# Retention's keys and values projected sooner; two gates and a query projected between the pairs of the lower half

## The chip, the core and the metric

The kernel runs on one core of a Trainium2 chip. The metric is the device time of one execution in microseconds (us), the median of several runs. The core has a matrix engine (TensorE, PE in the rows), three engines for element work (VectorE is DVE, ScalarE is ACT, GpSimd is POOL) and a queue from which most transfers are issued (SyncE, SP). Each engine works through its own instructions in the order in which they were built; an instruction that waits holds up all that stand behind it on that engine.

## The reference, cut to what matters

The input is x of 1024 rows by 1024 columns. It is normalised to u and multiplied with one wide weight matrix. The columns of the product are the inputs of three kinds of heads and of a gate:

```python
(dq, dk, dv, sq, ckv, iq, ik, iw, rq, rk, rv, gate) = jnp.split(proj, split_points, axis=-1)
o_a = diff_attention(dq, dk, dv, ...)        # 6 heads, difference of two softmaxes
o_b = dsa_attention(sq, rms_norm(ckv), iq, ik, iw, w_uk, w_uv, top_k)   # 6 heads, 256 best keys per query
o_c = retention(rotary(rq), rotary(rk), rv, ...)   # 4 heads, chunks of 128 rows with a running state
y = jax.nn.silu(gate) * concatenate([o_a, o_b, o_c])
h = h + y @ w_out;  return rms_norm(h, final_norm)
```

All is float32. The kernel multiplies in a reduced float format with both operands split into a high and a low part, so that each product takes three matmuls.

## The kernel before

**Projection units.** u lies in SBUF as `uh` and `ul` (high and low part, transposed). A unit projects a block of columns. It loads its weights from DRAM (tiles `wr`), GpSimd splits them into `wh` and `wl` (lines L119 and L123), and TensorE multiplies. The units of kind "b" (`g0` to `g7` for gates, `s0` to `s2` for the sparse queries, `q`, `k`, `ck`) have 48 matmuls of 512 columns (L130 to L132). The units `rq`, `rk`, `rv` of retention (kind "a") have 192 matmuls of 256 columns (L347 to L349). Results go back to DRAM: `gd` for gates, `qsq` for sparse queries, `rd` for retention; `rq` and `rk` are first rotated, two products on VectorE (L556, L557) and three on GpSimd (L559, L560, L563).

**Attention steps.** `attend` (L652) walks over 128-row blocks, one step each: scores on TensorE (L718 for differential attention, L787 and L788 for sparse), the row maximum on VectorE (L729, L795), the exponential on ScalarE, the division, transposes on TensorE (L678), their eviction on ScalarE (L113), and the product with the values on TensorE (L693). The steps are pipelined: scores of step t, transposes of step t-2. Differential attention has six sets of 8 steps (3 pairs of heads, 2 heads each). Sparse attention has, for each pair, 8 steps over the lower 512 rows (half 0) and 8 over the upper (half 1). `topk` and `ties` find the 256 best keys. One tie pass of a block is L490 to L495 on VectorE.

**Stages.** `run` (L898) makes four: the front; differential attention with `topk`, `ties` of blocks 3 and 2 and the units of `order` and `order2`; sparse attention over half 0 with the other ties, retention's blocks 0 to 3, the output weights and a first piece of the output projection; sparse attention over half 1 with retention's blocks 4 to 7 and two blocks of the output projection. The rest of the output projection ends the kernel.

**What sets the order.** `mix` (L46) interleaves streams by their costs and weights. What it makes is a priority: the tile scheduler then places each instruction by a simulated time line, so that matmuls of a unit and of the attention alternate finely. `order2` is a string of units; `M` stands for `up` and `ky` (values and keys of the sparse heads) mixed with the units of `mp`.

**Buffers that couple things.** The output weights `woh`, `wol` take the places of `uh`, `ul` (same tags, L964 and L965), so they can be written only when the last projection unit is through. Their 16 loads pass through two `wr` buffers, alternately split by ScalarE with VectorE and by GpSimd. The first projection piece (`project((7,), 0)`) needs `yr`, which SP loads too.

Of the kernel before, what the change touches and what calls it, by code (L numbers as in the profile page):

```python
# [28 lines left out]
    0, 384, 768, 1152, 1536, 1664, 2176, 2248, 2504, 2760, 3016)  # L29
WA = 384 + 72  # L30
C_R = (C_RQ, C_RK, C_RV)
K = {'mk': 'up ky', 'mp': 's2 g5 g4', 'rt': ('hl', 'pq'), 's0': ('gg', 'ag', 'gg', 'ag', 'gg', 'ag', 'gg', 'ag'), 'xp': 2, 'bufs': (8, 3, 3, 5, 3, 4, 1), 'pp': (7,), 'rot': 0, 'order': 'g0 g1 k1 q1 k2', 'order2': 'q2 g2 rq g6 s0 ck g7 s1 M g3 rv rk | ', 'wd': 36, 'wt': 13, 'wg': 119, 'gw': 56, 'rw': 26, 'rx': 132, 'pw': 40, 'ow': 84, 'nf': 2, 'ev': 200, 'late': 8, 'de': ('aa', 'aa', 'aa'), 'da': 'ax', 'gd': (7, 4, 2), 'hlp': 'sqkk', 'tkp': '', 'vt': 'v', 'rs': 'x', 'nv': 1, 'dn': 'v', 'ws': 'gg', 'oe': ('av', 'gg'), 'one': 0, 'idx': (42, 40), 'iqs': 'iq2 iq3 q0 k0'}
NST, NP, NPQ, NW, NHL, NHALF, NY = K["bufs"]


# [10 lines left out]
def mix(*streams):  # L46
    live = [[g, float(total), 0.0] for g, total in streams]
    while live:
        s = min(live, key=lambda v: v[2] / v[1])
        try:  # L50
            c = next(s[0])
            s[2] += c
            yield c
        except StopIteration:
            live.remove(s)


def interleave(*streams):
    for _ in mix(*streams):
        pass  # L60


def drain(*gens):
    for g in gens:
        for _ in g:
            pass


class Trunk:
# [260 lines left out]
    def evict(self, evac, *args):  # L330
        with self.tc.high_priority(offset=K["ev"]):
            evac(*args)
# [565 lines left out]
    def run(self):  # L898
# [24 lines left out]
        def seq(*gs):  # L923
            for g in gs:
                yield from g

        def units(s):
            return seq(*(unit(t) for t in s.split()))
# [4 lines left out]
        with self.tc.manual_schedule(engines={et.PE}):  # L933
# [6 lines left out]
                   (seq(self.topk(), self.ties((3, 2))), K["wt"]),  # L940
                   (units(K["order"] + " " + K["order2"].split("|")[0]), K["wg"]))
        self.v_load()
        interleave((seq(*(self.dsa(p, 0) for p in range(3))), 100), (self.ties((7, 6, 5, 4)), 110),
                   (seq(units(K["order2"].split("|")[1]), mix((self.retention(0), K["rw"]),
                                (seq(self.out_weights(), self.project(K["pp"], 0)), K["ow"]))), K["gw"]))
        interleave((seq(*(self.dsa(p, 1) for p in range(3))), 100),
                   (mix((self.retention(1), K["rx"]), (self.project(range(K["nf"])), 100)), K["pw"]))
        drain(self.project(range(K["nf"], 3)))
# [103 lines left out]
```

## Time and profile before

| | |
|---|---|
| median of 3 runs | 770.33 us (768.52 to 776.04) |
| profiled execution | 772.95 us, span 771.2 us, so 1.75 us lie outside the span |
| TensorE busy | 718.2 us (93%) |
| VectorE busy | 559.9 us (73%) |
| ScalarE busy | 458.6 us (59%) |
| GpSimd busy | 310.4 us (40%) |

A busy TensorE is not TensorE at its pace, since matmuls overlap in the records: one of 512 columns lasts 0.39 us there, while the next starts 0.23 us after it. What counts is how many starts a stretch has, and of what kind. The granted clock (1.00 is 2.4 GHz, and the lower level of 1.2 GHz pulls the mean down) stands beside each stretch.

### The profile page before, as it was taken

To read this page: it belongs to the slowest core of one execution; us is meant where nothing else is said; L and a number is where in the kernel's file an instruction comes from. 1 tells how busy PE (TensorE), PEld (TensorE's weight loads), DVE (VectorE), ACT (ScalarE), POOL (GpSimd) and SP (SyncE) were. 2 spreads that over 40 slices of the span, in tenths; PEclk is the share of its full clock that TensorE was granted. 3 is DMA by queue.
4 is the path that set the end of the run, shared out by engine and by line. 5 is a ranking of instruction groups with operands and counts; after the bars stand their busy time and mean duration, and the time that the engine had idled before them with its cause. 6 is when DMAs were issued, how large, how long until landed. Compare 5 with 4: busy or idle time off the path is not lost.

```text
span 771.2 us, 12824 instructions
## 1 busy us (share of the span) xinstructions
PE 718.2 (93%) x4266; PEld 591.1 (77%) x4266; DVE 559.9 (73%) x1315; ACT 458.6 (59%) x1002; POOL 310.4 (40%) x343
## 2 busy tenths in 40 slices
PE   6999999999989999978889889999978999999996
PEld 5986788887878988756767668989756887777884
DVE  3684577989999989999889986426657775654443
ACT  4762555489687877786845655533355665653332
POOL 6422122434424539447347787337633332120000
PEclk9999999999999999999899989999979999999998
DMA  9716455472484344451383685565579964413441
GB/s 337 255 28 178 137 159 142 111 191 79 118 202 109 99 132 113 114 144 31 91 239 108 172 229 167 145 203 165 177 212 272 251 203 113 132 34 106 137 166 55
DMA packets 93618, 116.73 MB, mean 151 GB/s; under 512 B 11120, under 2 KB 62704, under 8 KB 93424
## 3 DMA queue, kind: packets, MB, share of 16 engines
q1 hardware_dynamic: 91152, 111.94, 50.8%
q10 hardware_dynamic: 2400, 3.97, 1.4%
q8 instruction: 34, 0.56, 0.3%
q14 instruction: 32, 0.26, 0.1%
HBM read 79.17 MB, written 36.18 MB: 150 GB/s over the span
## 4 chain that ended last, share of the span: by engine, by line
PE 62%; DVE 13%; DMA 8%; issue 7%; ACT 4%; POOL 4%; SPq 2%; ACTq 0%; DVEq 0%; POOLq 0%
PE pG L130 6%; PE pG L131 6%; PE pG L132 6%; PE pB L693 5%; PE pB L678 4%; PE pG L1003 4%; PE pG L1004 4%; PE pG L1005 4%; PE pS L272 3%; PE pG L347 2%; DVE jv L443 2%; PE pG L349 2%; PE pG L348 2%; PE pS L409 2%; PE pS L408 2%
## 5 line engine op out<-in xcount | busy, mean ns | idle before, releaser
L130 PE MATMUL pG<-uh,wh 128*128 128x512 f32 x352 | 142.5, 405 | 4.5 <-DVE gt L894 2.1
L132 PE MATMUL pG<-uh,wl 128*128 128x512 f32 x352 | 141.2, 401 | 1.7 <-POOL wl L123 1.7
L131 PE MATMUL pG<-ul,wh 128*128 128x512 f32 x352 | 140.4, 399 | 1.3 <-DVE ul L255 1.3
L123 POOL TENSOR_TENSOR wl<-wr,wh 128x512 fp32r<-128x512 f32 x56 | 79.9, 1443 | 84.4 <-PE pG L131 73.8
L457 ACT ACTIVATE ja<-sc,tk_c 128x896 int8<-128x896 f32 (+2 forms) x93 | 83.3, 896 | 22.3 <-DVE tk_c L464 16.5
L113 ACT ACTIVATE pt<-pB 128x512 f32<-128x512 f32 (+2 forms) x120 | 58.9, 496 | 41.9 <-PE pB L678 41.7
L130 PEld LDWEIGHTS pG<-uh,wh 128*128 128x128 f32 x352 | 67.5, 192 | 19.3 <-DVE gt L894 2.4
L132 PEld LDWEIGHTS pG<-uh,wl 128*128 128x128 f32 x352 | 67.4, 192 | 16.7 <-POOL wl L123 2.5
L131 PEld LDWEIGHTS pG<-ul,wh 128*128 128x128 f32 x352 | 67.4, 191 | 15.5 <-DVE ul L255 3.3
L678 PE MATMUL pB<-ident,pp 128*128 128x128 f32 x432 | 73.4, 288 | 4.6 <-DVE gt L825 1.9
L693 PE MATMUL pB<-pt,v 128*64 128x128 f32 x864 | 68.0, 294 | 7.4 <-ACT pt L113 6.8
L693 PEld LDWEIGHTS pB<-pt,v 128*64 128x64 f32 x864 | 55.3, 143 | 18.9 <-ACT pt L113 9.5
L443 DVE TENSOR_SCALAR_CACHE_REDUCE jv<-sc,tk_c 128x640 bf16<-128x640 f32 (+4 forms) x81 | 69.1, 853 | 0.9
L119 POOL TENSOR_SCALAR wh<-wr 128x512 fp32r<-128x512 f32 x56 | 40.3, 723 | 69.9 <-DMA wr<-in_w_in_dram 50.8
L678 PEld LDWEIGHTS pB<-ident,pp 128*128 128x128 f32 x432 | 51.7, 145 | 20.4 <-issue 8.5
L744 POOL TENSOR_SCALAR pq<-pq,mx 128x896 f32<-128x896 f32 (+7 forms) x48 | 39.2, 816 | 58.5 <-DVE mx L743 46.1
L347 PE MATMUL pG<-wh,uh 128*128 128x256 f32 x192 | 55.4, 290 | 0.7 <-POOL wh L119 0.7
L411 ACT ACTIVATE pp<-pS 128x1024 f32<-128x1024 f32 (+5 forms) x48 | 36.5, 760 | 31.5 <-PE pS L409 31.5
L348 PE MATMUL pG<-wl,uh 128*128 128x256 f32 x192 | 55.0, 287 | 0.0
L349 PE MATMUL pG<-wh,ul 128*128 128x256 f32 x192 | 54.4, 284 | 0.0
L747 DVE SCALAR_TENSOR_TENSOR pp<-pp,mx,pq 128x896 f32<-128x896 f32 (+7 forms) x48 | 51.1, 1065 | 4.4 <-POOL pq L744 3.6
L416 DVE SCALAR_TENSOR_TENSOR sc<-pp,iw,sc 128x1024 f32<-128x1024 f32 (+5 forms) x42 | 43.5, 1048 | 14.6 <-ACT pp L411 14.2
(234 smaller groups left out, 1731.4 us busy)
## 6 DMA issues: line engine op xcount, KB each, us to landing
wr<-in_w_in_dram SPq DMA_DIRECT2D x56, 256.0 KB, 3.1
st<-qdq SPq DMA_DIRECT2D x24, 256.0 KB, 4.2
st<-qkk SPq DMA_DIRECT2D x18, 256.0 KB, 6.1
qiq<-hl SPq DMA_DIRECT2D x16, 256.0 KB, 3.5
st<-qiq SPq DMA_DIRECT2D x8, 512.0 KB, 3.4
wr<-in_w_out_dram SPq DMA_DIRECT2D x16, 256.0 KB, 3.3
xr<-in_x_dram SPq DMA_DIRECT2D x8, 512.0 KB, 3.6
yr<-yd SPq DMA_DIRECT2D x7, 512.0 KB, 4.1
```

The lines of the kernel that those rows point to most:

```text
L113: self.nc.scalar.activation(out, in_, AF.Copy)
L123: (self.nc.vector if e2 == "v" else self.nc.gpsimd).tensor_tensor(lo, src, hi.bitcast(F), OP.subtract)
L130: mm(ps, wh, xh, start=start, stop=False)
L131: mm(ps, wh, xl, start=False, stop=False)
L132: mm(ps, wl, xh, start=False, stop=stop)
L347: mm(ps, uh, hs[k], start=k == 0, stop=False)
L348: mm(ps, uh, ls[k], start=False, stop=False)
L349: mm(ps, ul, hs[k], start=False, stop=k == KC - 1)
L443: nc.vector.tensor_scalar(jv[:, :nv[b]], hb if b == 7 and bit >= 16 else sc[b], t, 0.0, op0=op, op1=OP.add, accum_out=cnt[:, j:j + 1])
L457: nc.scalar.activation(ja[:, :nv[b]], sc[b], AF.Sign, bias=cut(b), scale=-1.0, accum_out=cnt[:, cols[b]:cols[b] + 1])
L678: nc.tensor.transpose(p[:, k], pr[:, (k0 + k) * 128:(k0 + k + 1) * 128], self.ident)
L693: self.last = nc.tensor.matmul(o[u * 64:(u + 1) * 64], vals[k], pts[g, a][:, k, u * 128:(u + 1) * 128], start=k == (i if u else 0), stop=k ...
```

## The change

Three units leave the second stage and one table is written anew. In `order2` the second stage now has `q2 g2 rq s0 ck s1 M rk rv`, and `M` mixes `up ky` with `g3 g6 g7` (before: `s2 g5 g4`). The units `g4 s2` and `g5` now belong to the third stage. That stage, one call of `interleave` before, is now one call per pair of sparse heads: pair 0 with `g4 s2`, pair 1 with `g5`, pair 2 with nothing of the kind, each with a share of the ties and of retention's blocks; the output weights and the first piece of the projection come with pair 2. `rk` stands ahead of `rv` now.

```diff
-K = {..., 'mp': 's2 g5 g4', ..., 'order2': 'q2 g2 rq g6 s0 ck g7 s1 M g3 rv rk | ', ...}
+K = {..., 'mp': 'g3 g6 g7', ..., 'order2': 'q2 g2 rq s0 ck s1 M rk rv | g4 s2 | g5 | ', ...}
...
+def share(g, total):
+    while total > 0:
+        c = next(g, None)
+        if c is None:
+            return
+        total -= c
+        yield c
...
-        interleave((seq(*(self.dsa(p, 0) for p in range(3))), 100), (self.ties((7, 6, 5, 4)), 110),
-                   (seq(units(K["order2"].split("|")[1]), mix((self.retention(0), K["rw"]),
-                                (seq(self.out_weights(), self.project(K["pp"], 0)), K["ow"]))), K["gw"]))
+        ties, state = self.ties((7, 6, 5, 4)), self.retention(0)
+        side = K["order2"].split("|")[1:]
+        for p in range(3):
+            rest = mix((state, K["rw"]), (seq(self.out_weights(), self.project(K["pp"], 0)), K["ow"]))
+            interleave((self.dsa(p, 0), 33), (share(ties, 6), 30),
+                       (seq(units(side[p]), share(state, 4) if p < 2 else rest), 35))
+        drain(ties)
```

The built order shows what that makes. TensorE's instructions are the same as far as `rq`. Line numbers of the new kernel are 9 higher than before as far as `run` (13 higher in `project`). Before, TensorE went through the sparse steps of half 0 alone as soon as the last projection matmul (here at row 2252) was through; the scores are `pS`, the transposes take `ident`, the product with the values takes `pt` and `v`, and `rt` is retention's first block:

```order
2252 L349 MATMUL pG_5328<-wh_5085,ul 128x256
2253 L693 MATMUL pB_5796<-pt_5769,v_5586 64x128 x3
2254 L678 MATMUL pB_5820<-ident,pp_5778 128x128
2255 L787 MATMUL pS_5860<-st_5847,st_5848 128x512
2256 L788 MATMUL pS_5860<-st_5847,st_5848 128x512
2257 L787 MATMUL pS_5879<-st_5847,st_5848 128x128
2258 L788 MATMUL pS_5879<-st_5847,st_5848 128x128
2259 L678 MATMUL pB_5825<-ident,pp_5793 128x128 x2
2260 L693 MATMUL pB_5829<-pt_5819,v_5586 64x128 x3
2261 L678 MATMUL pB_5883<-ident,pp_5857 128x128 x3
2262 L787 MATMUL pS_5905<-st_5847,st_5848 128x256
2263 L788 MATMUL pS_5905<-st_5847,st_5848 128x256
```

Now the steps of pairs 0 and 1 have a unit between them; here it is the end of `g5`, with steps of pair 1:

```order
2268 L141 MATMUL pG_5957<-uh,wl_5796 128x512
2269 L139 MATMUL pG_5957<-uh,wh_5795 128x512
2270 L702 MATMUL pB_5854<-pt_5827,v_5367 64x128 x7
2271 L687 MATMUL pB_5885<-ident,pp_5836 128x128
2272 L796 MATMUL pS_5942<-st_5875,st_5876 128x128
2273 L797 MATMUL pS_5942<-st_5875,st_5876 128x128
2274 L140 MATMUL pG_5957<-ul,wh_5795 128x512
2275 L141 MATMUL pG_5957<-uh,wl_5796 128x512
2276 L139 MATMUL pG_5957<-uh,wh_5795 128x512
2277 L140 MATMUL pG_5957<-ul,wh_5795 128x512
```

After `g5`'s last matmul (row 2287) no unit is left, and TensorE has only the other steps and retention until the first matmul of the output projection (row 2413). In all, 123 matmuls of `g4`, `s2` and `g5` now stand between sparse steps, and 125 rows without a unit follow them.

VectorE, at the end of the fifth set of differential steps. Before, the last tie pass (L490 to L495, the block of 640 columns, `sc_665`) stood ahead of that set's last L747 (row 752):

```order
742 L490 TENSOR_SCALAR eq_5986<-sg_5985 128x640
743 L894 TENSOR_TENSOR gt_4294<-pG_4200,gt_4294 128x512
744 L491 SCALAR_TENSOR_TENSOR sc_665<-eq_5986 128x640
745 L745 RECIPROCAL mx_4260<-mx_4260 128x1
746 L492 TENSOR_SCALAR nd_5987<-nd_5987,sc_665 128x1
747 L746 TENSOR_SCALAR mx_4260<-mx_4260,nlam 128x1
748 L743 RECIPROCAL mx_4340<-mx_4340 128x1
749 L493 TENSOR_SCALAR nd_5987<-nd_5987 128x1
750 L494 SCALAR_TENSOR_TENSOR eq_5986<-sc_665,nd_5987,sg_5985 128x640
751 L495 TENSOR_SCALAR sc_664<-eq_5986 128x640
752 L747 SCALAR_TENSOR_TENSOR pp_4264<-pp_4264,mx_4260,pq_4261 128x256
```

Now that last L747 (L756 in the new numbering, row 738) comes first, and the end of one tie pass and the whole of the last stand behind it:

```order
738 L756 SCALAR_TENSOR_TENSOR pp_4325<-pp_4325,mx_4321,pq_4322 128x256
739 L503 SCALAR_TENSOR_TENSOR eq_5785<-sc_664,nd_5786,sg_5784 128x768
740 L523 TENSOR_TENSOR f_4122<-f_4122,f_4123 128x512
741 L504 TENSOR_SCALAR sc_664<-eq_5785 128x768
742 L499 TENSOR_SCALAR eq_5924<-sg_5923 128x640
743 L500 SCALAR_TENSOR_TENSOR sc_665<-eq_5924 128x640
744 L501 TENSOR_SCALAR nd_5925<-nd_5925,sc_665 128x1
745 L502 TENSOR_SCALAR nd_5925<-nd_5925 128x1
746 L503 SCALAR_TENSOR_TENSOR eq_5924<-sc_665,nd_5925,sg_5923 128x640
747 L504 TENSOR_SCALAR sc_664<-eq_5924 128x640
```

What moved is the work of about one and a half tie passes, from before to behind the end of that set.

SP, around the load of `yr` for the first piece of the output projection. Before, `yr` (row 314) was issued ahead of the last three loads of output weights (rows 315, 322, 324):

```order
311 L969 DMA wr_6068<-in_w_out_dram 128x512
312 L830 DMA yd_67<-gt_6146 128x1x128
313 L980 DMA fn_6215<-in_final_norm_dram 128x1024
314 L988 DMA yr_6217<-yd_68 128x3x128
315 L969 DMA wr_6072<-in_w_out_dram 128x512
316 L993 DMA xr_6219<-in_x_dram 128x1024
```

Now all 16 loads stand ahead of it, and the last six stand behind a store of pair 2's last product (row 316):

```order
316 L839 DMA yd_67<-gt_6286 128x1x128 x2
317 L982 DMA wr_6318<-in_w_out_dram 128x512
318 L392 DMA st_6781<-qkk_3914 64x1024
319 L982 DMA wr_6322<-in_w_out_dram 128x512
320 L392 DMA st_6781<-qkk_3914 64x1024
321 L982 DMA wr_6326<-in_w_out_dram 128x512
322 L982 DMA wr_6330<-in_w_out_dram 128x512
323 L982 DMA wr_6343<-in_w_out_dram 128x512
...
327 L982 DMA wr_6347<-in_w_out_dram 128x512
328 L993 DMA fn_6351<-in_final_norm_dram 128x1024
329 L1001 DMA yr_6353<-yd_68 128x3x128
```

What moved is the place of `yr` in the queue: three loads further back.

## Rows read from the trace of the kernel before

**Rows 1.** The page, busy time of each engine.

```profile
PE 718.2 (93%) x4266; PEld 591.1 (77%) x4266; DVE 559.9 (73%) x1315; ACT 458.6 (59%) x1002; POOL 310.4 (40%) x343
```

**Rows 2.** Windows: stretch and length, busy of PE, PEld, DVE, ACT, POOL, clock, DMA.

```profile
290.60:346.00 55.40, 48.78 (x274) 38.33 (x272) 52.93 (x133) 44.30 (x103) 35.21 (x38) 1.00 0.47 129
346.00:410.30 64.30, 56.15 (x296) 44.82 (x295) 57.85 (x150) 42.80 (x97) 30.66 (x34) 0.92 0.43 114
410.30:459.00 48.70, 42.80 (x229) 32.62 (x228) 45.94 (x91) 28.86 (x68) 43.37 (x35) 0.89 0.63 172
459.00:507.60 48.60, 47.71 (x345) 41.99 (x344) 23.59 (x65) 26.21 (x64) 22.06 (x25) 1.00 0.55 160
507.60:548.30 40.70, 39.80 (x315) 36.41 (x314) 20.81 (x58) 13.09 (x33) 26.26 (x35) 1.00 0.58 184
548.30:589.30 41.00, 33.61 (x211) 23.78 (x210) 27.20 (x92) 23.95 (x64) 14.64 (x16) 0.83 0.81 231
589.30:711.50 122.20, 119.63 (x914) 97.15 (x914) 78.35 (x174) 69.57 (x151) 30.90 (x42) 1.00 0.53 150
```

**Rows 3.** Timeline of PE where it runs undisturbed: start, length, instruction, count.

```profile
192.31 0.39 PE L130 MATMUL pG<-uh,wh 128*128 128x512 f32 x1
192.54 0.39 PE L131 MATMUL pG<-ul,wh 128*128 128x512 f32 x1
...
193.33 1.96 PE L693 MATMUL pB<-pt,v 128*64 128x128 f32 x30
195.22 0.66 PE L678 MATMUL pB<-ident,pp 128*128 128x128 f32 x4
195.63 0.71 PE L718 MATMUL pS<-st,st 128*128 128x512 f32 x2
...
536.01 0.28 PE L349 MATMUL pG<-wh,ul 128*128 128x256 f32 x1
536.12 0.28 PE L347 MATMUL pG<-wh,uh 128*128 128x256 f32 x1
```

**Rows 4.** Groups of VectorE by line, 346 to 459: busy, mean ns.

```profile
L491 DVE TENSOR_TENSOR_SCAN sc<-eq 128x512 f32<-128x512 bf16 (+5 forms) x6 | 11.0, 1826 | 0.0
L494 DVE SCALAR_TENSOR_TENSOR eq<-sc,nd,sg 128x512 bf16<-128x512 f32 (+5 forms) x6 | 7.2, 1197 | 0.1
L495 DVE TENSOR_SCALAR sc<-eq 128x512 bf16<-128x512 bf16 (+5 forms) x6 | 4.7, 789 | 0.1
```

**Rows 5.** Line L514 of VectorE (min/median/max ns); groups of POOL, 507.6 to 548.3.

```profile
L514 DVE TENSOR_TENSOR f<-f,f x6: 684/874/1780, 307.2 to 539.3; 128x512 f32<-128x512 f32 x6
...
L563 POOL TENSOR_TENSOR rt<-rt,trigdec 128x256 f32<-128x256 f32 x7 | 4.7, 675 | 0.2
L559 POOL TENSOR_TENSOR rt<-rt 128x128 f32<-128x128 f32 x7 | 3.6, 521 | 5.3 <-DVE rt L557 2.9 <-issue 2.3
```

**Rows 6.** Groups of PE by form, 548.3 to 589.3: busy, mean ns, idle before.

```profile
L678 PE MATMUL pB<-ident,pp 128*128 128x128 f32 x47 | 10.9, 344 | 2.1 <-DVE gt L825 1.9
L693 PE MATMUL pB<-pt,v 128*64 128x128 f32 x92 | 9.9, 325 | 0.5 <-ACT pt L113 0.5
L787 PE MATMUL pS<-st,st 128*128 128x512 f32 x10 | 5.5, 546 | 0.5 <-DVE mx L795 0.5
L788 PE MATMUL pS<-st,st 128*128 128x512 f32 x9 | 4.1, 453 | 1.2 <-DMA st<-qkk 1.2
```

**Rows 7.** Timeline of ACT: output weights split there, first, second and seventh.

```profile
548.31 0.63 ACT L113 ACTIVATE woh<-wr 128x512 fp32r<-128x512 f32 x1 [10.51 <-PE pG L348]
553.98 0.62 ACT L113 ACTIVATE woh<-wr 128x512 fp32r<-128x512 f32 x1
...
584.21 0.62 ACT L113 ACTIVATE woh<-wr 128x512 fp32r<-128x512 f32 x1
```

**Rows 8.** Timeline of SP and PE: `yr` issued, first matmul of the output projection.

```profile
582.28 0.46 SPq L988 DMA_DIRECT2D yr<-yd  x1
...
589.32 0.50 PE L1003 MATMUL pG<-woh,yh 128*128 128x512 f32 x1 [1.68 <-ACT yh L113]
```

More of the change, by code (lines that the diff above doesn't have):

```diff
@@ L31 @@
 C_R = (C_RQ, C_RK, C_RV)
-K = {'mk': 'up ky', 'mp': 's2 g5 g4', 'rt': ('hl', 'pq'), 's0': ('gg', 'ag', 'gg', 'ag', 'gg', 'ag', 'gg', 'ag'), 'xp': 2, 'bufs': (8, 3, 3, 5, 3, 4, 1), 'pp': (7,), 'rot': 0, 'order': 'g0 g1 k1 q1 k2', 'order2': 'q2 g2 rq g6 s0 ck g7 s1 M g3 rv rk | ', 'wd': 36, 'wt': 13, 'wg': 119, 'gw': 56, 'rw': 26, 'rx': 132, 'pw': 40, 'ow': 84, 'nf': 2, 'ev': 200, 'late': 8, 'de': ('aa', 'aa', 'aa'), 'da': 'ax', 'gd': (7, 4, 2), 'hlp': 'sqkk', 'tkp': '', 'vt': 'v', 'rs': 'x', 'nv': 1, 'dn': 'v', 'ws': 'gg', 'oe': ('av', 'gg'), 'one': 0, 'idx': (42, 40), 'iqs': 'iq2 iq3 q0 k0'}
+K = {'mk': 'up ky', 'mp': 'g3 g6 g7', 'rt': ('hl', 'pq'), 's0': ('gg', 'ag', 'gg', 'ag', 'gg', 'ag', 'gg', 'ag'), 'xp': 2, 'bufs': (8, 3, 3, 5, 3, 4, 1), 'pp': (7,), 'rot': 0, 'order': 'g0 g1 k1 q1 k2', 'order2': 'q2 g2 rq s0 ck s1 M rk rv | g4 s2 | g5 | ', 'wd': 36, 'wt': 13, 'wg': 119, 'gw': 56, 'rw': 26, 'rx': 132, 'pw': 40, 'ow': 84, 'nf': 2, 'ev': 200, 'late': 8, 'de': ('aa', 'aa', 'aa'), 'da': 'ax', 'gd': (7, 4, 2), 'hlp': 'sqkk', 'tkp': '', 'vt': 'v', 'rs': 'x', 'nv': 1, 'dn': 'v', 'ws': 'gg', 'oe': ('av', 'gg'), 'one': 0, 'idx': (42, 40), 'iqs': 'iq2 iq3 q0 k0'}
 NST, NP, NPQ, NW, NHL, NHALF, NY = K["bufs"]
```

## The prediction, on record before the changed kernel ran

> **What bounds the kernel now.** I read the page's busy times first, then the windows, then timelines. TensorE is busy for 718 of 771 us [rows 1], but that hides room, because matmuls overlap in the records. The pace is in the starts [rows 3]: 0.23 us from one 512-column matmul to the next (192.31 to 192.54), 0.12 us at 256 columns (536.01 to 536.12), 0.063 us for a record of L693 (1.89 us for 30) and 0.10 us for a transpose (0.41 us for 4). A unit of kind "b" is so 48 x 0.23 = 11.0 us of TensorE, one of retention's 192 x 0.12 = 23.0 us. The change adds no arithmetic, so the time moves only by what TensorE loses against this pace.
>
> The windows [rows 2] are cut at ends of sets of differential steps (346.0, 410.3, 459.0, 507.6), at the last projection matmul (548.3), at the first of the output projection (589.3) and at the last product with the values (711.5). Three kinds of stretch show. From 290.6 to 459.0 VectorE is busy for 156.7 of 168.4 us (93%), and TensorE waits for it. From 459.0 to 548.3 it is TensorE, 87.5 of 89.3 us at clock 1.00, with VectorE half idle. From 548.3 to 589.3 nobody is full: VectorE 27 of 41 us, clock 0.83. At pace the matmuls of those 41 us [rows 6] need 4.7 (47 transposes), 5.8 (92 of L693), 4.4 (19 scores of 512 columns), at most 4 (28 shorter scores) and 2 to 3 us (retention), some 21. So 20 us are lost there, because no projection unit is left between the sparse steps. By the same count 589.3 to 711.5 needs 110 of its 122 us.
>
> **The change, part by part.** All is the same as far as 290.6 us. I go by the built order and compare equal events.
>
> (1) 290.6 to the end of the fifth set of differential steps (459.0). TensorE loses work here (s2, g5 and half of g4 leave, g3 and a little of rk enter), but VectorE sets the time. Its order has, ahead of that set's end, one to two instructions fewer of each kind of a tie pass: 2.0 us of L491, 2.4 of L494, 2.3 of L495 and 0.6 of small ones, at the means of [rows 4]; also one gate product, one norm product and two row maxima, about 3 us. That is 10.5 us; at 93% busy some 9.5 us of time. **-9.5**; bounds 0 (the chain of a step sets the pace, not VectorE) and -10.5. The passes left over run in the next stretch, where VectorE has slack.
>
> (2) From there to the last product of differential attention (507.6). TensorE sets this. 24 matmuls of g4 and 48 of g3 leave, 166 of rk, 50 more of rv and 21 of g4 come: -51 x 0.23 + 216 x 0.12 = +14.2; half a microsecond for rv's second half of weights, which GpSimd splits just ahead of use. **+14.7**, so 63.3 us. VectorE gets 42 us of work here and GpSimd 49, both less than 63, so retention's rotation is hidden. If VectorE's slack of 21 us were gone, each further instruction would show.
>
> For the rotation there is a price to weigh. L514 with one shape took between 684 and 1780 ns in this part of the program, and the rotation's GpSimd operations last 0.52 us (L559), about as long (L560) and 0.68 us (L563) [rows 5]; before, the rotation of 7 of the second unit's 8 blocks ran beside a VectorE that was half idle [rows 2, 5]. The Trainium skill, "SBUF — State Buffer", section "Who interferes with whom", says that a VectorE instruction with two SBUF inputs and a GpSimd one that reads SBUF block each other for a whole instruction; the spread of L514 agrees. By that rule the 24 operations of rk could hold VectorE for 8 x 1.7 = 13.5 us; 42 + 13.5 is still below 63, so the sum is the same by rule and by row.
>
> (3) 507.6 to 589.3, 81.7 us before, becomes two parts. **(a)** to g5's last matmul: 123 matmuls of g4, s2, g5 at 0.23 = 28.3, and 13 to 14 us of other matmuls (24 scores, 28 transposes, 54 records of L693, one retention block, three norm matmuls), 42 at pace. With steps between a unit's matmuls as after 589.3, a tenth is lost, and a little more where four steps of pair 0 stand without a unit: **47.5**. **(b)** from g5's last matmul to the first of the output projection: 77 transposes, 62 scores, 148 records of L693 and two retention blocks, 35 us at pace. But the chain of output weights is longer. It starts when uh is free; before, the ScalarE splits came at 548.3, 554.0, ... 584.2, six cycles in 35.9 us, 6.0 each [rows 7]. `yr` was issued at 582.28, and the matmul it feeds began at 589.32 after a wait of 1.7 us [rows 8]: 7.0 us. Now the last load stands ahead of `yr`: six cycles 36, the load's buffer 2, two issues 1, then 7, so **47** instead of 41. TensorE's queue is in order, so every step behind the projection waits with it. Lower bound 43 (cycles of 5.4), upper 60.
> Together 94.5 for 81.7: **+12.8**.
>
> (4) From 589.3 to the end of the span, 181.9 us. Six of the 24 upper steps and two more retention blocks lie before this point now: 41 transposes (4.1), 27 scores (6), 82 records of L693 (5.2), 34 of retention and norm (6), with their tenth **-23.7**.
>
> Sum: -9.5 + 14.7 + 12.8 - 23.7 = -5.7. The profiled execution took 772.95 us, 771.2 in the span and 1.75 around it; it lies 2.6 above the median of the runs. Span after 765.5, own time 767.2, and on the median's footing 770.3 - 5.7 = **764.6**.
>
> **Rivals.**
> *More than that* (753.5). VectorE gives back all 10.5, (a) loses half, (b) takes 43, (4) loses one in fifteen: -1 -2.5 -4 -3.5. For: the clock was 1.00 wherever units were mixed in [rows 2]. Against: all four at once.
> *The change doesn't do what it says* (774). The fifth set ends no sooner, because the chain score, maximum, exponential, division sets it; then (1) is 0 and only the balance behind it stays, +3.8. For: VectorE idles for 6.5 us in 346.0 to 410.3. Against: 94 to 96% busy on both sides [rows 2].
> *The projection comes late* (785). On SP the last six loads stand behind the store of pair 2's last product. If the cycles take 9 us instead of 6, (b) is 47 + 7 x 3 = 68. Slower by over 1% from (b) above 60 us. For: DMA busy 0.81 in the stretch in which the loads ran [rows 2]. Against: six cycles of 6.0 under that load.
> *The clock falls* (788). If (b) ran at 1.2 GHz throughout, its 35 us are 70, 23 more. For: clock 0.83 in 548.3 to 589.3, after 507.6 to 548.3 at 1.00, when TensorE had only the steps. Against: 0.83 means a third of the stretch at the lower level, and that gives 41 here, hidden under the chain's 47. The Trainium skill, "TensorE: Matmul & The Clock Gate", section "HAM oscillation — how this bites in real kernels", says that bursts with waits between them run at the lower clock again and again; the 0.83 agrees in part, and by that rule in full the time is this rival's.
>
> **How the numbers follow.** A measurement here tells about 1% (7.7 us) from no change: faster is below 762.6, slower above 778.0. Forecast 0.52, its own range 757 to 772, of which 0.25 below 762.6. More than that 0.16. No gain in (1) 0.14, of which 0.03 above 778. Projection late 0.13, clock 0.05, both slower. So faster 0.25 + 0.16 = 0.41, same 0.27 + 0.11 = 0.38, slower 0.03 + 0.18 = 0.21. The range takes in the forecast, the better case, no gain and the milder late projections: 752 to 780.
>
> **What would show it.** (1) The fifth set ends near 449.5 us, and the stretch ahead of it still has VectorE above 90%. (2) The last product of differential attention comes near 513, TensorE busy throughout, VectorE near two thirds. (3) g5's last matmul near 560, no gap above 2 us ahead of it; the first matmul of the output projection near 607, released by `yh`, with output weights split every 6 us before it. (4) The rest takes 158 us. Wrong would be: the fifth set at 459 (VectorE wasn't the bound); more than 4 us of waiting at rv's weights; (b) above 55 us, with SP standing at a store.

## The result, and the profile after

The changed kernel takes 794.74 us (median of three runs, 792.37 to 796.05) against 770.33; the ratio is 1.0297, with a 95% interval of 1.0253 to 1.0341. 764.6 was forecast, in a range of 752 to 780, and faster. It went 24 us the other way.

The profiled execution has a span of 793.0 us, 21.8 more than before. The page's busy times, which answer to [rows 1]:

```profile
PE 726.9 (92%) x4266; PEld 595.5 (75%) x4266; DVE 560.9 (71%) x1314; ACT 456.9 (58%) x1003; POOL 310.6 (39%) x343
```

No engine has more to do. TensorE's busy time is 8.7 us longer with the same 4266 matmuls: a matmul is recorded longer where it waits or runs at the lower clock (0.99 us instead of 0.39 for one of 512 columns, in a line further down). The windows of after, cut at the same events as [rows 2] (ends of the third to sixth set of differential steps, `g5`'s last matmul, the first matmul of the output projection, the last product with the values; columns as there):

```profile
287.90:344.40 56.50, 49.28 (x262) 36.89 (x261) 55.02 (x137) 43.93 (x102) 41.41 (x43) 0.94 0.46 116
344.40:393.30 48.90, 43.63 (x248) 34.59 (x245) 43.89 (x127) 35.00 (x85) 19.36 (x22) 0.93 0.50 136
393.30:457.80 64.50, 49.64 (x259) 38.64 (x256) 62.95 (x115) 36.08 (x83) 48.39 (x41) 0.84 0.54 158
457.80:522.60 64.80, 63.49 (x512) 58.55 (x509) 25.14 (x80) 20.22 (x57) 34.77 (x47) 1.00 0.35 102
522.60:576.50 53.90, 49.94 (x265) 38.52 (x262) 23.60 (x64) 23.15 (x55) 22.03 (x23) 0.91 0.58 180
576.50:634.40 57.90, 45.99 (x346) 35.44 (x345) 40.63 (x104) 35.05 (x84) 19.79 (x22) 0.91 0.74 222
634.40:729.30 94.90, 93.06 (x686) 74.49 (x686) 58.02 (x129) 52.45 (x112) 18.84 (x28) 1.00 0.45 132
```

From the end of `rq` to the end of the fifth set it is 169.9 us (168.4 before), although 12 us of matmuls less stand in it; then 64.8 (48.6), 53.9 + 57.9 = 111.8 (81.4) and 158.6 (181.9): +1.5 + 16.2 + 30.4 - 23.3 = +24.8. The stretch ahead, where TensorE's instructions are the same, took 287.9 instead of 290.9 us (it ends between 286.3 and 290.9 in all twenty traces read below, so this is taken as chance), which leaves the 21.8 of the spans.

**A ledger.** One number makes the twenty kernels below comparable. Every matmul is priced at the start-to-start interval that its line and shape had undisturbed before (the 30th percentile there; those of [rows 3] are 0.23, 0.12, 0.063, 0.10). From the end of `rq` to the last matmul this sum is 391.0 us in before, in after and in every kernel that leaves nothing out. What a stretch takes beyond the sum of its matmuls is lost to TensorE. Each kernel's row is one profiled execution, and executions of one kernel lie up to 11 us apart (e8: 808.67 to 819.28), so a difference of a few us in one row alone says little.

| lost, us | to the fifth set | to the sixth | to the last unit's end | from there on | all |
|---|---|---|---|---|---|
| before | 41.8 | 3.6 | 3.9 | 32.2 | 81.5 |
| after | 55.2 | 6.0 | 12.4 | 32.8 | 106.4 |

The gain was to come from the last column but one: sparse steps with units between them were to lose less. It didn't move. Before, all units were through at 548.1 us and the rest lost 32.2; now they are through at 576.3, seven of the lower half's twelve products with the values follow instead of ten, and the rest loses 32.8. Nearly all of the 25 us lie ahead of that, 13.4 of them in the stretch in which VectorE sets the time.

### The profile page after: what moved, and what is told of

The parts are those of the page before. It is cut to its first block, busy times and chain, and to the rows that moved or that the text cites. A ratio compares the mean times of both kernels' runs of the same rounds, so it can differ in the third digit from the quotient of the medians.

```text
span 793.0 us, 12845 instructions
## 1 busy us (share of the span) xinstructions
PE 726.9 (92%) x4266; PEld 595.5 (75%) x4266; DVE 560.9 (71%) x1314; ACT 456.9 (58%) x1003; POOL 310.6 (39%) x343
## 3 DMA queue, kind: packets, MB, share of 16 engines
q1 hardware_dynamic: 91152, 111.94, 48.6%
## 4 chain that ended last, share of the span: by engine, by line
PE 58%; DVE 13%; DMA 11%; issue 6%; POOL 5%; ACT 4%; SPq 1%; ACTq 0%; DVEq 0%; POOLq 0%
PE pG L139 6%; PE pG L140 6%; PE pG L141 6%; PE pB L702 4%; PE pG L1017 4%; PE pG L1016 4%; PE pG L1018 4%; PE pB L687 3%; PE pS L281 3%; DVE pp L756 2%; DMA wr<-in_w_in_dram 2%; PE pG L356 2%; DVE jv L452 2%; DMA wr<-in_w_out_dram 2%; PE pS L418 2%
## 5 line engine op out<-in xcount | busy, mean ns | idle before, releaser
L140 PEld LDWEIGHTS pG<-ul,wh 128*128 128x128 f32 x352 | 67.8, 193 | 15.6 <-DVE ul L264 3.2
L139 PEld LDWEIGHTS pG<-uh,wh 128*128 128x128 f32 x352 | 67.8, 192 | 15.6 <-POOL wl L132 1.6
L702 PEld LDWEIGHTS pB<-pt,v 128*64 128x64 f32 x864 | 55.6, 144 | 16.3 <-ACT pt L122 6.2
L753 POOL TENSOR_SCALAR pq<-pq,mx 128x896 f32<-128x896 f32 (+7 forms) x48 | 40.8, 851 | 66.6 <-DVE mx L752 57.7
L727 PE MATMUL pS<-st,st 128*128 128x512 f32 (+3 forms) x144 | 45.5, 386 | 12.3 <-DVE mx L738 9.5
L357 PE MATMUL pG<-wl,uh 128*128 128x256 f32 x192 | 55.1, 288 | 0.0
L425 DVE SCALAR_TENSOR_TENSOR sc<-pp,iw,sc 128x1024 f32<-128x1024 f32 (+5 forms) x42 | 44.2, 1062 | 13.5 <-ACT pp L420 13.1
```

What stands on the lines that cost most here:

```text
L139: mm(ps, wh, xh, start=start, stop=False)
L140: mm(ps, wh, xl, start=False, stop=False)
L357: mm(ps, uh, ls[k], start=False, stop=False)
L702: self.last = nc.tensor.matmul(o[u * 64:(u + 1) * 64], vals[k], pts[g, a][:, k, u * 128:(u + 1) * 128], start=k == (i if u else 0), stop=k ...
```

## The experiments

Ratios are to runs of the kernel before on the same chip, with 95% intervals; a hundredth is 7.7 us. The last five columns are the ledger.

| | ratio | interval | to fifth | to sixth | to last unit | after | all |
|---|---|---|---|---|---|---|---|
| after | 1.0297 | 1.0253-1.0341 | 55.2 | 6.0 | 12.4 | 32.8 | 106.4 |
| e1 split alone | 1.0042 | 1.0009-1.0074 | 42.2 | 4.6 | 3.6 | 37.3 | 87.6 |
| e2 moved, no split | 1.0282 | 1.0254-1.0311 | 56.2 | 4.6 | 2.2 | 41.7 | 104.8 |
| e5 split, new order | 1.0103 | 1.0060-1.0145 | 52.8 | 2.2 | 4.6 | 34.1 | 93.7 |
| e6 split, g5 moved | 1.0220 | 1.0184-1.0256 | 42.3 | 9.1 | 12.3 | 37.6 | 101.3 |
| e17 after, old order | 1.0237 | 1.0185-1.0290 | 54.3 | 3.1 | 10.9 | 31.5 | 99.9 |
| e18 before, late gates | 1.0040 | 1.0020-1.0061 | 48.3 | 2.0 | 2.3 | 34.2 | 86.7 |
| e11 after, rv first | 1.0271 | 1.0233-1.0309 | 55.7 | 3.3 | 10.4 | 35.1 | 104.5 |
| e3 after, ties held | 1.0229 | 1.0209-1.0249 | 47.1 | 6.2 | 12.4 | 34.0 | 99.7 |
| e7 before, ties held | 0.9966 | 0.9942-0.9989 | 37.2 | 2.0 | 9.0 | 31.6 | 79.9 |
| e4 after, five buffers | 1.0253 | 1.0228-1.0278 | 55.6 | 5.5 | 10.6 | 31.7 | 103.4 |
| e12 e7, five buffers | 1.0063 | 1.0033-1.0093 | 33.3 | 3.5 | 10.1 | 37.6 | 84.5 |
| e8 after, weights late | 1.0534 | 1.0475-1.0593 | 56.4 | 5.4 | 13.3 | 55.1 | 130.2 |
| e9 before less g4 | 1.0062 | 1.0033-1.0090 | 44.5 | 8.6 | 4.8 | 42.1 | 99.9 |
| e10 after less g4 | 1.0162 | 1.0129-1.0194 | 54.1 | 5.8 | 12.6 | 32.4 | 104.9 |
| e13 e9, rv rk held | 1.0158 | 1.0110-1.0206 | 43.9 | 19.7 | 11.3 | 32.8 | 107.7 |
| e14 after, rk rv held | 1.0388 | 1.0343-1.0433 | 56.7 | 14.6 | 16.5 | 28.6 | 116.4 |
| e15 before, rv rk held | 1.0219 | 1.0179-1.0260 | 41.5 | 13.5 | 11.3 | 37.5 | 103.8 |
| e16 e15, ties held | 1.0124 | 1.0095-1.0152 | 34.6 | 12.8 | 11.9 | 34.1 | 93.5 |

### Which part of the change costs

e1 is the kernel before with the third stage in pairs; e2 the changed table with the third stage in one call.

```diff
 e1:  before, with share() and the loop over pairs
-'order2': '... s1 M g3 rv rk | '
+'order2': '... s1 M g3 rv rk | | | '
 e2:  after, with the third stage of before
-'order2': '... M rk rv | g4 s2 | g5 | ', 'gw': 56
+'order2': '... M rk rv | g4 s2 g5', 'gw': 180
```

> The kernel before with one part of the change: the third stage is called once per pair of sparse heads, with shares of ties and retention and with the output weights in pair 2, but no unit is moved, and the table of units is the old one. Two theories of the 22 us that the change lost. V, VectorE's sum: VectorE sets the time from 291 to 459 us whatever TensorE has to do there, so three units taken out of that stretch save nothing there and cost their 28 us later; the split itself is nearly free. Then this kernel ends stage two like the kernel before (fifth set near 459, last projection matmul near 548) and takes 768 to 778. S, the split: output weights that start only with pair 2 and sparse steps without cover cost the time; then this kernel takes 785 to 797, with more than 55 us from the last projection matmul to the first of the output projection.

> The changed kernel's table of units (g4, s2, g5 in the third stage, g3, g6, g7 in M, rk ahead of rv) with the third stage in one call as before, the side stream at a weight of 180 instead of 56, so that the three units come in time. V, VectorE's sum: as slow as the changed kernel, 788 to 797, with the fifth set of differential steps at 455 to 460 and VectorE above 95% ahead of it. S, the split: near the kernel before, 768 to 778.

V, by both times (774.39 and 792.67): the split costs 3.2 us (0.7 to 5.7), and the new table costs the rest with or without it. Next, the order of the table without any unit leaving, and one unit leaving without the order:

```diff
 e5:  e1, 'mp': 'g3 g6 g7'
+'order2': 'q2 g2 rq s0 ck s1 M s2 g5 g4 rk rv | | | '
 e6:  e1, 'mp': 's2 g4'
+'order2': 'q2 g2 rq g6 s0 ck g7 s1 M g3 rv rk | | g5 | '
```

> The third stage in pairs as in the changed kernel, and the changed table's new order (g6 and g7 in M behind g3's place, rk ahead of rv), but s2, g5 and g4 stay in the second stage, ahead of rk. No unit is moved out. V, the moved units are what costs: 770 to 778, like the kernel with the split alone (774.4). O, the order costs (gates of retention later, rk ahead of rv): 783 to 795.

> The kernel with the split alone and one unit moved: g5 goes to pair 1 of the third stage, s2 and g4 stay in the second. V says that each 11 us unit taken out of the stretch in which VectorE sets the time is paid later, less what it hides between sparse steps (2 to 4 us): 11 - 3 = 8 us more than 774.4 at most, a third of the 18 us between the split alone and the changed kernel at least: 779 to 783. If the first one moved is free (TensorE has slack enough behind it): 772 to 776.

e5 fell between the two expectations: the order costs 4.7 us (1.0103 against 1.0042, with an error of 4 us). e6 missed both of its expectations: one unit is not a third of the loss but most of it, 13.7 us (error 4) of the 19.6 between e1 and after. The windows of e1 to the fifth and the sixth set, then those of e6 (to the fifth set, to the sixth, to `g5`'s last matmul, and within that from `rk`'s last to `g5`'s first):

```profile
286.50:455.20 168.70, 147.57 (x800) 115.19 (x799) 156.72 (x369) 116.81 (x266) 108.20 (x105) 0.95 0.49 135
455.20:504.70 49.50, 47.65 (x348) 41.94 (x344) 23.36 (x65) 25.82 (x63) 22.33 (x26) 1.00 0.55 160
...
287.80:451.00 163.20, 139.40 (x774) 108.10 (x773) 152.76 (x359) 112.49 (x261) 108.60 (x104) 0.97 0.49 134
451.00:510.10 59.10, 55.00 (x408) 49.82 (x405) 32.94 (x84) 29.89 (x73) 25.47 (x27) 0.97 0.50 146
510.10:566.30 56.20, 52.07 (x353) 43.72 (x350) 28.28 (x75) 16.96 (x44) 30.63 (x44) 0.94 0.52 164
536.90:551.30 14.40, 11.57 (x84) 8.19 (x82) 10.68 (x32) 7.87 (x23) 6.95 (x9) 0.87 0.59 179
```

The first stretch is 5.5 us shorter than e1's 168.7, the second 9.6 longer than e1's 49.5 (`rv` now stands in it from 465 us, in e1 from 481), and then there is a hole: `rk` is through at 536.8, but `g5` belongs to pair 1 and begins at 551.3, with sparse steps and retention's first block alone between. In the ledger 8.7 of the 13.7 us lie in the stretch with the hole and 4.5 in the sixth set's. Two more runs took the order apart from the units:

```diff
 e17: after, 'mp': 'g3'
+'order2': 'q2 g2 rq g6 s0 ck g7 s1 M rv rk | g4 s2 | g5 | '
 e18: before, 'mp': 's2 g5 g4 g6 g7'
+'order2': 'q2 g2 rq s0 ck s1 M g3 rv rk | '
 e11: after
+'order2': 'q2 g2 rq s0 ck s1 M rv rk | g4 s2 | g5 | '
```

> The changed kernel with g6 and g7 back at their old places (ahead of s0, and behind ck) and rv ahead of rk; M mixes up and ky with g3 alone, and g4, s2, g5 stay in the third stage. G (the gates' place): with g6 and g7 late, TensorE lost 55 us instead of 42 from 288 us to the fifth set's end, in e5 too, where no unit is moved out; with them early it should lose 42 to 46 there, and the whole take 782 to 788. N (fewer units ahead of the fifth set): the loss stays at 52 or more there, and the whole at 790 to 797.

> The kernel before with g6 and g7 moved into M, behind s2, g5 and g4; nothing else. G: the stretch to the fifth set loses 50 to 57 us of TensorE instead of 42, and the whole takes 777 to 785. N: 769 to 775.

> The changed kernel with rv ahead of rk again. rk began at 444.6 us, ahead of the fifth set's end, where VectorE was 98% busy, and its rotation asks VectorE for two products and GpSimd for three for each 24 matmuls; rv's results need a copy on ScalarE alone. If the order of these two makes the new table slow (it cost 5.5 us in all, e5 against e1): the fifth set ends 3 to 6 us sooner and the whole takes 788 to 791. If not: 793 to 797.

e17 has the time that G expected and the loss that N expected: 54.3 us to the fifth set, with the gates early. So late gates are not why that stretch loses 13 us more in after; e18, with the time that N expected, gives them 6.5 of the ledger and 3.1 us of time. `rv` first (e11) is worth 2 us, inside the error, and the fifth set ends no sooner for it. The sums agree from two sides, each with an error of 4 to 5 us: order 4.7 (e5 less e1) and 4.6 (after less e17, by itself not clear of nothing); three units moved 14.9 (after less e5) and 15.0 (e17 less e1). The split is 3.2.

### What VectorE holds up

```diff
 e3 on after, e7 on before, in ties():
+with self.tc.issue_after(self.dlast.ins) if b > 3 else ExitStack():
     nc.scalar.activation(sg, pre, AF.Sign, ...)
     nc.vector.tensor_scalar(eq, sg, 0.0, 1.0, ...)
...
```

`dlast` is the last division of differential attention; the four upper tie passes then stand behind it on VectorE.

> The changed kernel with one thing more: the tie passes of the four upper blocks (1024, 896, 768 and 640 columns), which nothing needs before the fourth stage, are queued on VectorE behind the last division of differential attention. V, VectorE's sum: some 22 us of VectorE leave the stretch to the fifth set, which ends 15 to 22 us sooner (436 to 443 instead of 457.6); the next stretch has room for them, so the last product of differential attention comes near 505 and the whole takes 772 to 782. A rival, the chain: scores, maximum, exponential, division of a step set the pace of the sets and VectorE is busy only by the way; then the fifth set stays within 4 us of 457 and the whole at 789 to 797.

> The kernel before, with the tie passes of the four upper blocks queued on VectorE behind the last division of differential attention; nothing else. In the changed kernel this brought the fifth set 9 us forward and the whole 5 to 8. V: the same stretch of the kernel before (291 to 459 us, VectorE 93% busy) shrinks by 5 to 9 us, and the whole takes 761 to 766. If TensorE's larger share of work there (12 us more than in the changed kernel) leaves no room: 767 to 771.

e3 lands between its theories: counted from the end of `rq` the fifth set ends 8 us sooner (161.8 for 169.9) and not 15 to 22; the whole takes 788.56. Its windows from the end of `rq` and from the fourth set to the fifth, then e7's from the end of `rq`:

```profile
286.80:448.60 161.80, 141.20 (x760) 108.85 (x759) 139.82 (x350) 111.98 (x262) 102.10 (x104) 0.92 0.52 140
392.60:448.60 56.00, 47.12 (x259) 36.41 (x256) 40.33 (x88) 32.86 (x76) 41.30 (x40) 0.91 0.59 168
...
286.90:457.10 170.20, 152.76 (x829) 120.51 (x828) 145.22 (x361) 118.08 (x270) 105.84 (x111) 0.95 0.52 142
```

VectorE falls from 98% (62.95 of 64.50) to 72%, so it did set the time there, but only for 8 us; below that something else does, which no run here isolates. In e7 the stretch to the fifth set stayed at 170.2 us, with 133.0 of TensorE's work in it instead of 126.6, and the sixth set came after 40.6 instead of 48.6. e7's time, 769.05, is that of its second expectation; it is the only kernel here that is faster than before, by 0.34% (0.11 to 0.58).

The other traces say the same of VectorE. In the fourteen kernels without held tie passes, other than e5 and e18, it is busy for 92 to 96% of the stretch from the end of `rq` to the fifth set, and the length of that stretch goes with VectorE's work and not with TensorE's: VectorE has 153 us to do where it takes 163 to 165 (e6, e9, e13), and 157 to 163 us where it takes 168 to 172 (all others); TensorE's matmuls need 121 us in the first three and 112 to 127 in the others. In e5 and e18, with late gates and every unit, the share is 90%, with the passes held 85 to 87%.

### What a unit costs

```diff
 e9 on before ('mp': 's2 g5'), e10 on after ('| s2 | g5 | '): g4 is not projected
+self.gd.setdefault(4, self.gd[c]) if c == 3 else None
```

> The kernel before with one unit left out of the second stage: g4 isn't projected, and pair 1 of the sparse heads reads pair 0's gate in its place. It measures what a unit of 11 us costs in the stretch in which VectorE sets the time. V (units stand in VectorE's shadow there): 1 to 5 us less than the kernel before, 766 to 770. P (TensorE's work counts wherever it stands): 9 to 12 us less, 759 to 762.

> The changed kernel with the same unit left out: g4 no longer stands between the sparse steps of pair 0. It measures what the unit costs there. Forecast of the change's own idea (units fill the gaps between sparse steps): 2 to 5 us less than the changed kernel, 789 to 793. V (there TensorE sets the time and a unit is paid nearly in full): 8 to 11 us less, 783 to 787.

e10 is V's number: between sparse steps the unit costs 10.4 us (1.0297 less 1.0162, with an error of 4) of its 11; no hiding shows. e9 is beyond both expectations: with 11 us less to multiply the kernel before is 4.8 us slower. Its windows to the fifth and the sixth set, and from `rk`'s end to the last product with the values:

```profile
287.80:453.20 165.40, 141.35 (x774) 110.76 (x773) 152.99 (x359) 112.39 (x261) 108.57 (x104) 0.95 0.49 132
453.20:511.90 58.70, 53.48 (x409) 48.28 (x406) 32.68 (x84) 29.66 (x73) 26.00 (x27) 1.00 0.51 147
...
539.40:715.60 176.20, 158.42 (x1156) 125.11 (x1155) 114.19 (x285) 98.12 (x228) 50.01 (x62) 0.94 0.57 168
```

The first gives back 3 us of 11, with 3.7 us less for VectorE to do; then `rv` begins 14 us sooner (179.5 from the end of `rq`, before 193.6) and the sixth set's stretch takes 58.7 instead of 48.6; and `rk` is through 6 us sooner (251.6, before 257.2), with more sparse steps behind it and more lost from there on (42.1 instead of 32.2). That the one makes the other is not shown; the next four runs tried it.

### Was retention too early?

e9 suggested a theory F: `rk` and `rv` pulled forward hold up the sixth set and no longer stand between the sparse steps. Held behind the last product of differential attention (`dav`), they should undo the loss.

```diff
 e15 on before, e16 with e7's edit, e13 on e9, e14 on after ('M | rk rv g4 s2 | g5 | ')
-'order2': '... M g3 rv rk | '
+'order2': '... M g3 | rv rk'
+with self.tc.issue_after(self.dav.ins) if self.dav else ExitStack():
     mm(ps, uh, hs[k], start=k == 0, stop=False)
...
```

> The kernel before without g4, as in e9 (776.7 us, 4.7 more than the kernel before, with 11 us less work), and with rv and rk queued on TensorE behind the last product of differential attention. F (retention pulled forward): e9 is slow because rv came 17 us sooner, into the stretch of the sixth set, which grew from 48.6 to 58.6 us while the sparse steps lost the cover. With rv and rk held behind it, that stretch falls to 35 to 45 us and the whole takes 758 to 768. Rival, the sparse steps alone: what e9 lost comes from the 29.5 us that TensorE waits in the lower half, whatever stands in the sixth set's stretch: 773 to 779.

> The changed kernel with rk and rv queued on TensorE behind the last product of differential attention (they stand in the third stage's stream of pair 0, ahead of g4 and s2). F: the sixth set's stretch falls from 64.8 to 40 to 48 us, retention's 46 us of matmuls and the three units then all stand beside sparse steps, and most of the loss of 22 us is gone: 772 to 782. Rival: TensorE's sum from there on is the same wherever the matmuls stand: 790 to 797.

> The kernel before with rv and rk held in the same way and nothing else changed. F: the sixth set's stretch of 48.6 us loses some 15 us of rv's matmuls, which come to stand beside sparse steps that had no cover: 760 to 768. If the kernel before has rv and rk at the right place already: 769 to 776.

> The kernel before with rv and rk held, and the four upper tie passes held on VectorE as in e7 (3.3 us less by itself). If both gains add up: 756 to 764. If the tie passes then collide with the rotation of rv's and rk's neighbours and the sparse steps on VectorE: 766 to 774.

F falls in all four: the sixth set came sooner as it said (43.9, 26.3, 43.0 and 35.2 us behind the fifth) and every kernel became slower, slower also than its second expectation (783.71, 800.66, 789.09 and 781.11 us). e15's windows, from the fifth set on:

```profile
455.00:498.00 43.00, 36.35 (x215) 28.07 (x212) 25.86 (x74) 24.96 (x61) 22.59 (x26) 0.95 0.59 175
498.00:575.50 77.50, 75.29 (x603) 67.69 (x601) 36.15 (x119) 28.94 (x83) 26.47 (x35) 0.96 0.53 163
575.50:718.10 142.60, 128.00 (x919) 99.22 (x918) 87.24 (x182) 73.78 (x158) 45.01 (x58) 0.93 0.51 148
```

The sixth set saves 6 us but loses 13.5 of TensorE (before: 3.6). Counted from the end of `rq` the lower half is through 3 us sooner (292.1, before 295.5), but the last unit 31 us later (288.5, before 257.2); only then can the output weights be written, and the first projection matmul comes at 337.4 instead of 298.4. In the upper half TensorE loses 36 us (before: 14), and the gain is gone.

### The output weights

```diff
 e4 on after, e12 on e7, in out_weights():
-raw = self.rtile([512])
+raw = self.sb.tile([128, 512], F, name=self.name("wr"), tag="w", bufs=NW)
 e8 on after: out_weights() moved to the start of the fourth stage, 'pp': ()
```

> The changed kernel with the 16 raw output weights loaded through the five buffers of the w ring, which is empty by then, instead of two buffers. The stretch from the last matmul of g5 to the first of the output projection took 57.9 us. C, the chain: loads that come late hold the splits on ScalarE and VectorE (8.4 us of ScalarE's waits for them), and the steps' evictions and maxima stand behind those splits; then the splits no longer wait, the stretch takes 42 to 50 us for the same steps, and the whole is 780 to 787. R, the steps alone: without a unit beside them the sparse steps go no faster; then it stays at 790 to 797.

> The changed kernel with the output weights and the first piece of the projection taken out of the third stage; they come at the start of the fourth, where the two blocks of the projection wait for them (block 7 is projected whole at the end). It shows what the chain of output weights costs the sparse steps of the lower half. C, the chain costs them: the lower half's last set ends near 597 instead of 607.1. R, the steps' own chain, with TensorE's queue in order, sets it: 604 to 607. The whole: 785 to 800, by how much of the fourth stage the later chain then holds up.

> The kernel before with both mends that helped singly: the four upper tie passes behind the last division of differential attention (3.3 us less, e7), and raw output weights through the five buffers of the w ring (3 to 4 us less in the changed kernel, e4). If both add up: 764 to 767. If the loads aren't late there (the stretch in question has other gaps to fill): 768 to 771.

ScalarE's waits for raw weights behind `g5`, in after and then in e4 (total, times, longest):

```profile
ACT woh L122 <- DMA wr<-in_w_out_dram: 8.4, 6, 3.1
```

```profile
ACT woh L122 <- DMA wr<-in_w_out_dram: 3.7, 4, 2.9
```

With five buffers the waits fall by 4.7 us and the first projection matmul comes 39.4 instead of 58.1 us behind the last unit, but TensorE loses as much from there on as in after (31.7, 32.8), and the time falls by 3.4 us, inside an error of 4. So the chain of output weights was not what held the sparse steps; the time, 790.56, is R's. On the kernel before the same edit, with the ties held, made things worse by 7 us (e12 against e7: 1.0063, 0.9966), beyond both expectations; why is open. e8 bounds the other side, and it too is beyond both. Without any weights in the third stage the lower half ends at 616.4 us, not sooner than 607.1; why later is not shown. Then TensorE waits 9 us at the projection's first matmul,

```profile
PE pG L1016 <- ACT yh L122: 9.1, 1, 9.1
```

and the whole is 18 us slower than after. So no run shows a cost of loading the weights beside the sparse steps, and loading them later costs more.

## Why the prediction was wrong, point by point

The forecast of -5.7 us was off by 30.5: 11.0 in (1), 1.5 in (2), 17.6 in (3) and 0.4 in (4).

**(1), to the end of the fifth set, -9.5: this step failed.** Measured +1.5. VectorE did reach the set's last division sooner, as its order says: at 442.06 us, 154.2 behind the end of `rq`; before it was through at 456.0, 165.1 behind it. Those 10.9 us are what the prediction had counted (10.5). But it cut VectorE's order there, and let "the passes left over run in the next stretch". Before, the set's last product with the values followed 3 us behind that division (VectorE, then TensorE):

```profile
454.52 1.50 DVE L747 SCALAR_TENSOR_TENSOR pp<-pp,mx,pq 128x256 f32<-128x256 f32 x1
...
459.04 0.65 PE L693 MATMUL pB<-pt,v 128*64 128x128 f32 x6
```

Now the passes left over ran at once, ahead of it (timeline of VectorE: the last division, the last tie pass, and the next row maximum):

```profile
441.27 0.79 DVE L756 SCALAR_TENSOR_TENSOR pp<-pp,mx,pq 128x256 f32<-128x256 f32 x1
...
444.04 1.13 DVE L499 TENSOR_SCALAR eq<-sg 128x640 bf16<-128x640 bf16 x1 [0.18 <-ACT sg L498]
445.20 2.45 DVE L500 TENSOR_TENSOR_SCAN sc<-eq 128x640 f32<-128x640 bf16 x1
...
448.13 1.86 DVE L503 SCALAR_TENSOR_TENSOR eq<-sc,nd,sg 128x640 bf16<-128x640 f32 x1
450.02 1.27 DVE L504 TENSOR_SCALAR sc<-eq 128x640 bf16<-128x640 bf16 x1
451.21 1.08 DVE L738 CUSTOM_DVE_ANT_0 pq<-pS,cb 128x896 f32<-128x896 f32 x1
```

The row maximum belongs to the sixth set. On TensorE further scores of that set stand ahead of the last transposes of the fifth, and they waited for this maximum (timeline of TensorE: `rk`'s first matmul, scores of the sixth set, transposes and last product of the fifth):

```profile
444.63 0.36 PE L356 MATMUL pG<-wh,uh 128*128 128x256 f32 x1 [2.88 <-ACT hl L373]
...
452.35 1.22 PE L727 MATMUL pS<-st,st 128*128 128x512 f32 x2 [2.03 <-DVE mx L738]
...
455.29 0.39 PE L687 MATMUL pB<-ident,pp 128*128 128x128 f32 x2
...
457.57 0.65 PE L702 MATMUL pB<-pt,v 128*64 128x128 f32 x6
```

So the passes left over still lay ahead of the set's last product, which came 15.5 us behind the division. The bound was named rightly (VectorE 95% busy to the fifth set, 161.9 of 169.9 us; e3). What was wrong is how much VectorE had to do up to the event that ends the set: not 10.5 us less than before but 5.1 more (161.9 for 156.7). The 12 us of matmuls taken from TensorE there gave nothing back: 114.8 us of them took as long as 126.6.

**(2), 63.3 us: right in what TensorE needs.** 64.8, TensorE at clock 1.00 throughout. VectorE has 25 us to do and not 42; 8.4 of the 17 are the passes, which were done, and for the rest the prediction gives no working. It didn't matter: TensorE set the time, busy for 63.5 of the 64.8 us, so the rotation held nobody up.

**(3a), 47.5 us: too small by 6.** 53.9, of which the hole between `s2` and `g5` has most. The prediction knew that steps stand there without a unit and priced them at "a little more" than a tenth. Timeline of TensorE: the last of `s2`, retention's first matmul, the first of `g5`:

```profile
545.39 0.39 PE L141 MATMUL pG<-uh,wl 128*128 128x512 f32 x1
...
551.67 0.33 PE L596 MATMUL pG<-ident,rt 128*128 128x128 f32 x1 [1.67 <-DMA rt<-rd]
...
560.99 0.99 PE L139 MATMUL pG<-uh,wh 128*128 128x512 f32 x1
```

These 15.6 us hold 6.9 of work. No single gap is above 2 us, as was said; the rest is small gaps, longer intervals and a clock of 0.78 (545.4 to 561.0). "No gap above 2 us" was no test of the loss. Nor is the hole the whole price: e2 has none (2.2 us lost to the last unit's end) and loses 9 us more than after behind it (41.7), with nearly the same time.

**(3b), 47 us: too small by 11, and its chain was miscounted.** 57.9. Timeline of ScalarE, the first, second and eighth of its splits, then `yh`; of SP, `yr`; of TensorE, the first projection matmul:

```profile
577.26 0.62 ACT L122 ACTIVATE woh<-wr 128x512 fp32r<-128x512 f32 x1
...
589.04 0.62 ACT L122 ACTIVATE woh<-wr 128x512 fp32r<-128x512 f32 x1
...
625.38 0.63 ACT L122 ACTIVATE woh<-wr 128x512 fp32r<-128x512 f32 x1 [0.43 <-DMA wr<-in_w_out_dram]
...
633.83 0.52 ACT L122 ACTIVATE yh<-yr 128x384 fp32r<-128x384 f32 x1 [1.54 <-DMA yr<-yd]
```

```profile
627.14 0.43 SPq L1001 DMA_DIRECT2D yr<-yd  x1
```

```profile
634.40 0.50 PE L1016 MATMUL pG<-woh,yh 128*128 128x512 f32 x1 [0.16 <-ACT yh L122]
```

With all 16 loads ahead of `yr` ScalarE makes eight splits and so seven cycles, not the six that the prediction took over from before; they took 48.1 us (577.26 to 625.38), 6.9 each, the first 11.8 since its load stood behind a store and retention's transfers on SP. From `yr` on it was 7.3 us (forecast 7.0). But the chain is not the reason of the loss: e4 brought the projection 19 us forward and gained 3.4. TensorE waited 0.16 us for `yh`; the steps ahead of it took that long. The mis-sized term is theirs: the prediction gave 47 us to 35 us of matmuls and took the chain as what fills them, but steps without a unit lost 23 us here, as they had lost 20 before.

**(4), 158.2 us: right** (158.6).

**The picture behind the sum.** The prediction read the 20 us lost from 548.3 to 589.3 as work for a unit to fill. Two things spoke against it. `rv` and `rk` already stood between sparse steps (507.9 to 548.1, 3.9 us lost): before, 242 of their matmuls, 29 us, covered these; after, 123 of `g4`, `s2` and `g5`, 28 us, do, with a hole, because retention now lies beside the sixth set. The cover didn't grow. And the steps that are left behind the last unit lose as much as before, though they are fewer; it is 28.6 to 42.1 us in all kernels but e8.

**The rivals.** "Doesn't do what it says" had the right place (the fifth set ends no sooner) and gave it 3.8 us, because the 17.6 us of (3) were not in it. Its reason was wrong, and so was the sign "the fifth set at 459 (VectorE wasn't the bound)": the set ended at 457.8 with VectorE at 95%. "The projection comes late" named a chain that is late but isn't the cause. "The clock falls" was placed in (b), where the clock was 0.91 (before 0.83); it fell to 0.84 in the stretch that VectorE sets. At the lower level matmuls of 512 columns start 0.43 us apart instead of 0.23 (before, clock 0.5):

```profile
449.09 0.63 PE L131 MATMUL pG<-ul,wh 128*128 128x512 f32 x1
449.52 0.63 PE L132 MATMUL pG<-uh,wl 128*128 128x512 f32 x1
```

Time at 1.2 GHz to the fifth set, from the clock of each window, is 21 us before and 34 after; the matmuls begun in it have 8.4 and 13.2 us of work, so by its matmuls' own length it could add at most 5 of the 13 us lost there. The Trainium skill, "TensorE: Matmul & The Clock Gate", section "HAM oscillation — how this bites in real kernels", says that bursts with waits between them run at the lower clock again and again; the windows agree where TensorE waits for VectorE (0.84), and no run here holds the clock up to price it.

**Open.** The parts of the loss are measured (split 3, order 5, moved units 15 us, each with an error of 3 to 5). Not settled is why one moved unit costs nearly as much as three (e6), and which wait keeps the loss behind the last unit near 30 to 40 us whatever is left there. e3 and e4 show only that the upper tie passes are worth about 5 and the late raw weights about 3 us of the whole, each with an error of 4.

## What to carry to other kernels

In a stretch that another engine sets, look at that engine's work: here 12 us of matmuls taken out of it gave nothing back, and one unit between the sparse steps cost nearly its full price in spite of the gaps there (e10). Taking a unit out of the first stretch even cost (e9). Before a gap is filled, price the stretch as a sum of starts and look at what leaves it: here as much cover left (`rv`, `rk`) as came in. And cut two engines' orders at the same event: a division that comes sooner on VectorE is no gain until TensorE's queue, in its order, reaches the product that needs it.

## What was not expected of the hardware

Less work made the program slower: without `g4` the kernel before takes 4.8 us more (1.0062, 1.0033 to 1.0090); the order in which the engines' queues then meet is another, and which wait costs the time is open. In the kernel before, VectorE's L514, two inputs and one shape, took 0.68 and 0.69 us where no GpSimd instruction ran beside it, and 0.77 to 1.78 us in the four cases where one did. And the granted clock differed with nearly the same matmuls, though not all in the same order: it is 0.84 in after from 393.3 to 457.8 us, where they lose 27.5 us to waits and clock, and 0.91 in e3 from 392.6 to 448.6, where VectorE has less to do and they lose 19.1.
